# Chunked delta-rule scan in a diffusion step: second adaLN stage in another PSUM bank, chunk tiles without zeros, group norm squares on other engines

## Chip, cores and metric

One core of one Trainium2 chip runs the whole program. The metric is the device time of one execution in microseconds (us), lower is better; the median of three runs of the kernel before is given.

## What is computed

One inference step of a trunk of two layers over 128 context tokens and 512 latent tokens, width 1024. Layer 0 mixes tokens by a bidirectional delta-rule scan (RWKV-7) with 16 heads of 64, layer 1 by neighbourhood attention; behind each stands an MLP with squared ReLU. Every sub-layer is scaled, shifted and gated by six vectors (adaLN) that a matrix product makes from a conditioning vector. The scan, per head and direction, and what follows it:

```python
def step(S, inp):
    r_t, w_t, k_t, v_t, kk_t, a_t = inp
    sa = jnp.einsum('bhvk,bhk->bhv', S, -kk_t)
    S_new = (S * w_t[:, :, None, :] + sa[..., None] * (kk_t * a_t)[:, :, None, :]
             + v_t[..., None] * k_t[:, :, None, :]).astype(S.dtype)
    y = jnp.einsum('bhvk,bhk->bhv', S_new, r_t)
    return S_new, y
...
y = (ys[0] + ys[1]).astype(jnp.float32)
mean = jnp.mean(y, axis=-1, keepdims=True)
var = jnp.mean(jnp.square(y - mean), axis=-1, keepdims=True)
yn = ((y - mean) * lax.rsqrt(var + GN_EPS)).reshape(B, T, D) * ln_w + ln_b
...
sh1, sc1, gt1, sh2, sc2, gt2 = ada_mod(cond, ada_w[l], ada_b[l])
```

## The kernel before

The scan works in chunks of 32 tokens and holds 4 chunks of 5 blocks (one of context, four of latent tokens) for two directions d = 0, 1. `phase_scan` (from L770) loops over the blocks n and over four chunk steps e; in each, chain 0 and chain 1 advance by one chunk (`chain_step`, L1001), and between their parts `fill` (L881) slips in the preparation of a later block.

Preparation. For one unit (a block, one of two head groups hg, a direction, one of two windows) `prep_elem` (L899) loads decays and keys, sums the decays (L916, `wi`, on DVE, which is VectorE), takes two exponentials (L917, L918, ACT, which is ScalarE) and multiplies on POOL (GpSimd): KB, the write keys, and C (L947), the read keys. C has 128 partitions, 64 for each head of a pair (h = 0, 1); for head h the slots 8h to 8h+7 are filled on its own 64 partitions, and on the other 64 partitions they are set to zero (L939 on ACT for h = 1, L942 on POOL for h = 0). Slots 16 and 17 of C hold a 128x128 identity that `c_slots` (L728) writes once for each of the 16 C tiles. `prep_group` (L949) multiplies KB with C and the identity, 16 products to a group, two groups to a unit, into the PSUM tile `pp` (L852 is `mm`, which issues all products of the scan and chains them in program order). Then ACT copies a part to invA (L972) and the transposed write keys to C (L974), and DVE masks the rest into the zeroed half of C (L977), so that C can be multiplied over all 128 partitions. With eight units of a block done, `invert` (L979) inverts 32 triangular matrices at a time on DVE: a transpose (L985), 50 multiplications (L993) and 50 additions (L996), a transpose into TT (L998).

Chain. A chunk step is R = C x state into bank A (L852), copied by ACT to Rc (L1035); U = TT x Rc into bank A, copied by ACT into the state's tile GU (L1052); the state's update into bank B and its copy back to GU by ACT (L1108) or DVE with a decay (L1106, L1111); Y = C x GU into bank A, copied by ACT (L1069) or added by DVE (L1067). Each chain has one bank A, so R, U and Y of a chain use it one after the other. Each step also takes one block of 256 columns of the adaLN product: `ada_first` (into `pp`, copied to `adasb` at L289), and `ada_second` (L1046 calls it), two products of 2 columns and one DVE addition (L300, `mods`). They go to columns 256 to 259 of U's bank A of chain 1.

```python
        if self.ada_sums and d == 1:
            self.ada_second(*self.ada_sums.pop(0), ut[:, 256:260], self.mm)
        with tc.high_priority():
            for pp in range(2):
                for hp in range(2):
                    q = 2 * hp + pp
                    nc.scalar.activation(gu[64 - 64 * hp:96 - 64 * hp, hp, pp].rearrange("p b v -> p (b v)"),
                                         U[32 * q:32 * q + 32, :], AF.Copy, scale=-0.5)
```

Behind the chains `post_half` (L1114) normalises half a block of Y: mean (L1136) and subtraction (L1139), squares (L1140, ACT), their sum (L1142), an inverse root and the rest (L1146 to L1151) on DVE or POOL, whichever `el` is, a transpose on TensorE and two DVE products (L1160). `pbuf`, in which the squares lie, has one buffer for each pool; its other parts are loaded and stored by DMA.

The order of TensorE's instructions in the scan is the program's own; on the other engines a scheduler places them when the kernel is built, so that an edit moves rows on all engines.

Of the kernel before, what the change touches and what calls it, by code (L numbers as in the profile page):

```python
# [8 lines left out]
F32 = mybir.dt.float32  # L9
F32R = mybir.dt.float32r  # L10
I32 = mybir.dt.int32
AF = mybir.ActivationFunctionType
ALU = mybir.AluOpType
# [3 lines left out]
P = 128  # L17
# [155 lines left out]
class K:  # L173
# [554 lines left out]
    def c_slots(self, pool, n, par):  # L728

        for i in range(n):  # L730
            c = pool.tile([P, 26, 64], F32, name=f"C{i}")
            self.nc.any.tensor_copy(c[:, 16:18, :].rearrange("p a x -> p (a x)"), self.cst("ident"))
            self.free[par].append(c)
# [166 lines left out]
    def prep_elem(self, ts, hg, d, i):  # L900
# [34 lines left out]
        C = ts["C"][d, hg, ww] = self.free[ts["par"]].pop(0)  # L935
        for h in range(2):
            z = C[64 - 64 * h:P - 64 * h, 8 * h:8 * h + 8, :]
            if h:
                nc.scalar.activation(z.rearrange("p a b -> p (a b)"), self.cst("scan1")[64 - 64 * h:P - 64 * h, :512],  # L939
                                     AF.Copy, scale=0.0)  # L940
            else:
                nc.gpsimd.memset(z, 0.0)  # L942
        for s, f in ((0, f_at), (1, f_rt)):
# [5 lines left out]
    def prep_group(self, ts, hg, d, i, e):  # L949

        nc = self.nc
        ww = (i, 1 - i)[d]
        KB, C = ts["KB", hg, d, i], ts["C"][d, hg, ww]
        if e == 0:
            self.pa = self.pp_tile()
        pa = self.pa
        pv = pa.rearrange("p (e q x) -> p e q x", e=2, q=4)
        for q in range(4):
            for h in range(2):
                n = 8 * h + 4 * e + q  # L960
                r = 64 - 64 * h
                self.mm(pv[r:r + 64, e, q, :], lhsT=KB[:, q, e].rearrange("p s t -> p (s t)"), rhs=C[:, n:17 + h:16 + h - n, :],
                        start=True, stop=True, tile_position=(0, r))
        if e == 0:
            return
        if "D" not in ts:
            ts["D"] = self.inv.tile([P, 2, 8, 2, 32], F32, name="invA")
        mask = self.cst(f"amask{d}").unsqueeze(1).broadcast_to([P, 8, 64])
        pn = pa.rearrange("p (n x) -> p n x", x=P)
        for h in range(2):  # L970
            for b in range(2):
                nc.scalar.copy(ts["D"][32 * (2 * h + b):32 * (2 * h + b) + 32, d, 4 * hg + 2 * ww:4 * hg + 2 * ww + 2],  # L972
                               pv[64 - 64 * h:96 - 64 * h, :, b:4:2, 0:32])
        nc.scalar.copy(C[:, 18:26, :], pn[:, :, 64:P])  # L974
        for h in range(2):
            o = slice(64 - 64 * h, P - 64 * h)
            nc.vector.tensor_tensor(C[o, 8 * h:8 * h + 8, :], pn[o, :, 0:64], mask[o], op=ALU.mult)  # L977
# [23 lines left out]
    def chain_step(self, ts, n, e, d):  # L1001
# [21 lines left out]
        def state_product(s):  # L1023
            ps = self.ch.tile([P, 512], F32, name=f"A{d}")[:, :256]
            for ph, pp, hp in idx:
                q = 2 * hp + pp
                i = 8 * hp + 4 * ee + 2 * (ph % 2) + pp
                self.mm(ps[32 * q:32 * q + 32, 64 * ph:64 * ph + 64], lhsT=C[ph // 2][:, i, 32 * s:32 * s + 32],
                        rhs=gu[:, hp, pp, ph, :], start=True, stop=True, tile_position=(0, 32 * q))
            return ps  # L1030

        R = state_product(0)
        with tc.high_priority():
# [3 lines left out]
        TT = ts["TT"]  # L1037
        ut = self.ch.tile([P, 512], F32, name=f"A{d}")
        U = ut[:, :256]
        for ph, pp, hp in idx:  # L1040
# [4 lines left out]
                    rhs=Rc[qs, o], start=True, stop=True, tile_position=(32 * q, 32 * q))  # L1045
        if self.ada_sums and d == 1:  # L1046
            self.ada_second(*self.ada_sums.pop(0), ut[:, 256:260], self.mm)
        with tc.high_priority():
# [9 lines left out]
        yield  # L1058
        Y = state_product(1)
        tt = ts["tiles"][d]  # L1060
        with tc.high_priority():
            if tt not in self.yt:
                self.yt[tt] = self.yp.tile([P, 4, 256], F32, name="Y")
                self.ydone[tt] = set()
            yo = self.yt[tt][:, cq, :]
            if cq in self.ydone[tt]:
                nc.vector.tensor_tensor(yo, yo, Y, op=ALU.add)  # L1067
            else:
                nc.scalar.copy(yo, Y)  # L1069
                self.ydone[tt].add(cq)  # L1070
        if e % 2 == 1:
            self.free[ts["par"]] += [ts["C"].pop((d, hg, ww)) for hg in range(2)]
        yield

    def state_update(self, ts, n, e, d, gu, nx, C):
# [13 lines left out]
        for pp in range(2):  # L1089
            for ph in range(4):  # L1090
                for hp in range(2):
                    i = 18 + 4 * ee + 2 * (ph % 2) + pp
                    self.mm(G[hs(hp), pp, ph, :], lhsT=C[ph // 2][ho(hp), i, :], rhs=gu[ho(hp), hp, pp, ph, :],
# [20 lines left out]
    def post_half(self, tt, hb, on_dve):  # L1114
# [24 lines left out]
        el.tensor_tensor(Yg, Yg, bcast(sm), op=ALU.subtract)  # L1139
        nc.scalar.activation(sq, Yg, AF.Square)  # L1140
        var = po.tile([P, 8], F32, name="yvar")
# [456 lines left out]
```

## Time and profile before

| what | us |
|---|---|
| median of three runs | 2232.8 (2231.12 to 2234.78) |
| profiled execution | 2239.71 |
| its span, first to last instruction | 2237.9 |
| TensorE busy | 2011.6 (90%) |
| VectorE busy | 1169.5 (52%) |
| ScalarE busy | 857.0 (38%) |
| GpSimd busy | 455.1 (20%) |

The mean granted TensorE clock is 0.944. Preparation for the scan begins at about 288 us, the chains run from 400 to some 790 us, the output projection of the scan ends at some 842 us, and the rest is matrix products of MLP and attention. The busy times are sums over the whole span; where the scan's time goes is seen only by stretches.

### The profile page before, as it was taken

What the parts mean: (1) busy time and instruction counts of PE and PEld (TensorE: products, weight loads), DVE (VectorE), ACT (ScalarE), POOL (GpSimd) and SP (SyncE); (2) the same over time, 40 slices, a digit from 0 to 9 for tenths busy, and PEclk for the clock granted to TensorE, in tenths of its full rate; (3) what the DMA queues carried; (4) which work ended last, traced back from release to release, by engine and by line L of the source; (5) the groups of instructions that cost most, each with busy time, mean ns of one, the idle gap of its engine ahead of it and who ended that gap; (6) DMA issues with size and microseconds to landing.
All of it is one profiled execution on the core that took longest, in us unless ns stands there. A gap on an engine that the chain in (4) does not pass through costs nothing.

```text
span 2237.9 us, 44938 instructions
## 1 busy us (share of the span) xinstructions
PE 2011.6 (90%) x18604; PEld 1827.3 (82%) x18604; DVE 1169.5 (52%) x2592; ACT 857.0 (38%) x1712; POOL 455.1 (20%) x553
## 2 busy tenths in 40 slices
PE   6999988757665569999999999999999999999999
PEld 3777777646554568999999998889677999999999
DVE  6656658387679755433333434433666633434342
ACT  4544553546553414313131323221576331313130
POOL 0001275656542411101010110000232110101010
PEclk8997999978787788999999999999899999999999
DMA  6455764545433464323232223343310232222221
GB/s 242 147 157 155 229 205 135 173 133 166 129 132 96 112 187 141 105 76 111 72 111 76 86 76 119 132 135 92 110 57 31 75 122 76 76 76 76 76 74 69
DMA packets 161037, 260.03 MB, mean 116 GB/s; under 512 B 46528, under 2 KB 102976, under 8 KB 160832
## 3 DMA queue, kind: packets, MB, share of 16 engines
q1 hardware_dynamic: 152224, 244.05, 35.2%
q10 hardware_dynamic: 8608, 13.11, 1.7%
q8 instruction: 146, 2.39, 0.4%
q14 instruction: 59, 0.48, 0.1%
HBM read 218.18 MB, written 37.35 MB: 114 GB/s over the span
## 4 chain that ended last, share of the span: by engine, by line
PE 74%; DVE 13%; DMA 5%; POOL 3%; issue 2%; ACT 2%; SPq 1%; DVEq 0%; ACTq 0%; POOLq 0%
PE psl L205 54%; PE psl L239 3%; DVE invX L996 2%; PE ps L1525 2%; DVE invT L993 2%; POOL C L947 2%; PE po L1562 2%; PE pp L852 2%; PE pt L1550 2%; DVE C L977 1%; PE pp L1219 1%; PE psl L1265 1%; PE psl L286 1%; DMA ld_s<-scr 1%; PE A L852 1%
## 5 line engine op out<-in xcount | busy, mean ns | idle before, releaser
L191 ACT CAST whi<-wraw 128x1024 fp32r<-128x1024 f32 x178 | 186.6, 1049 | 731.5 <-PE psl L205 701.9
L205 PE MATMUL psl<-xh,whi 128*128 128x320 f32 (+1 forms) x1696 | 414.6, 317 | 9.6 <-ACT xh L247 4.9
L205 PE MATMUL psl<-xl,whi 128*128 128x320 f32 (+1 forms) x1696 | 410.2, 314 | 1.2 <-DVE xl L248 1.2
L205 PE MATMUL psl<-xh,wlo 128*128 128x320 f32 (+1 forms) x1696 | 409.7, 314 | 0.4 <-DVE ta L592 0.4
L205 PEld LDWEIGHTS psl<-xh,whi 128*128 128x128 f32 x1696 | 291.4, 191 | 28.5 <-issue 8.7
L205 PEld LDWEIGHTS psl<-xl,whi 128*128 128x128 f32 x1696 | 292.5, 191 | 5.7 <-issue 3.2
L205 PEld LDWEIGHTS psl<-xh,wlo 128*128 128x128 f32 x1696 | 292.9, 191 | 2.6 <-issue 1.7
L1172 DVE SCALAR_TENSOR_TENSOR xres<-psl,mods,xres 128x320 f32<-128x320 f32 (+2 forms) x216 | 81.7, 434 | 305.1 <-PE psl L205 305.1
L1345 POOL TENSOR_TENSOR relu<-relu 128x640 f32<-128x640 f32 x64 | 80.2, 1255 | 773.9 <-ACT relu L1344 758.7
L205 PE MATMUL psl<-hhl,whi 128*128 128x320 f32 x1024 | 233.1, 308 | 0.0
L205 PE MATMUL psl<-hhh,wlo 128*128 128x320 f32 x1024 | 233.0, 308 | 0.0
L205 PE MATMUL psl<-hhh,whi 128*128 128x320 f32 x1024 | 232.9, 308 | 0.0
L193 DVE TENSOR_TENSOR wlo<-wraw,whi 128x1024 fp32r<-128x1024 f32 x178 | 218.6, 1229 | 11.6 <-ACT whi L191 10.9
L205 PEld LDWEIGHTS psl<-hhh,whi 128*128 128x128 f32 x1024 | 170.8, 188 | 0.4 <-issue 0.4
L205 PEld LDWEIGHTS psl<-hhh,wlo 128*128 128x128 f32 x1024 | 171.1, 188 | 0.0
L205 PEld LDWEIGHTS psl<-hhl,whi 128*128 128x128 f32 x1024 | 171.0, 188 | 0.0
L1302 DVE TENSOR_TENSOR relu<-psl,rms_b 128x320 f32<-128x320 f32 x128 | 60.8, 486 | 144.6 <-PE psl L205 144.0
L852 PE MATMUL pp<-C,KB 128*64 128x128 f32 x1280 | 100.6, 306 | 39.7 <-DVE C L977 16.7
L852 PEld LDWEIGHTS pp<-C,KB 128*64 128x64 f32 x1280 | 83.0, 154 | 54.1 <-issue 28.8
L248 DVE TENSOR_TENSOR hhl<-relu,hhh 128x640 fp32r<-128x640 f32 x64 | 53.4, 834 | 127.9 <-ACT hhh L247 127.7
L1052 ACT ACTIVATE GU<-A 32x256 f32<-32x256 f32 x160 | 60.0, 375 | 93.2 <-DVE mods L300 64.0
L977 DVE TENSOR_TENSOR C<-pp,cstsb 64x512 f32<-64x512 f32 x80 | 55.0, 688 | 69.1 <-ACT C L974 56.9
(299 smaller groups left out, 3393.2 us busy)
## 6 DMA issues: line engine op xcount, KB each, us to landing
wraw<-in_mlp_w SPq DMA_DIRECT2D x128, 512.0 KB, 3.5
adaraw<-in_ada_w SPq DMA_DIRECT2D x96, 512.0 KB, 4.9
ld_d<-scr SPq DMA_DIRECT2D x20, 512.0 KB, 4.5
ld_s<-scr SPq DMA_DIRECT2D x20, 512.0 KB, 3.7
bias<-in_bias SPq DMA_DIRECT2D x16, 384.0 KB, 3.7
scr<-ta SPq DMA_DIRECT2D x16, 325.0 KB, 3.5
wi<-scr SPq DMA_DIRECT2D x20, 260.0 KB, 4.6
scr<-bp SPq DMA_DIRECT2D x16, 320.0 KB, 4.5
```

Source lines behind the costliest of these rows:

```text
L191: nc.scalar.copy(hi, raw)
L193: nc.vector.tensor_tensor(lo, raw, hi.bitcast(F32), op=ALU.subtract)
L205: self.nc.tensor.matmul(ps[g][:, :e - c], lhsT=a[:, k, :], rhs=b[:, c:e], start=(k == 0 and j == 0), stop=(k == n - 1 and j == 2))
L239: nc.tensor.matmul(ps, lhsT=a[:, tc_], rhs=w, start=(k == 0 and j == 0), stop=(k == KT - 1 and j == 2))
L248: (lo_eng or nc.vector).tensor_tensor(xl, src, xh.bitcast(F32), op=ALU.subtract)
L852: r = (op or self.nc.tensor.matmul)(*a, **k)
L947: nc.gpsimd.tensor_tensor(rev(o) if s == 0 else o, v4(sh, s, ww)[hs], f[hs], op=ALU.mult)
L977: nc.vector.tensor_tensor(C[o, 8 * h:8 * h + 8, :], pn[o, :, 0:64], mask[o], op=ALU.mult)
L1052: nc.scalar.activation(gu[64 - 64 * hp:96 - 64 * hp, hp, pp].rearrange("p b v -> p (b v)"), U[32 * q:32 * q + 32, :], AF.Copy, scale=-0.5)
L1172: nc.vector.scalar_tensor_tensor(out[:, a:b], ps[g][:, o:o + b - a], gate[:, k, j:j + 1], x[:, a:b], op0=ALU.mult, op1=ALU.add)
L1302: nc.vector.tensor_tensor(t[:, c], ps[q][:, :HALF], rb[:, c], op=ALU.mult)
L1345: nc.gpsimd.tensor_tensor(t, t, t, op=ALU.mult)
```

## The change

Four edits. (1) `ada_second` is called after Y, and its products go to columns 256 to 259 of Y's bank A; it was called after U. (2) C loses the zeroed halves: the ACT and POOL instructions that wrote them go, and the chunk products of head h run over the 64 partitions of h alone (`KB[hs]`, `C[hs]`), with the tile's row position 64h beside its column position. The mask's result (L977) is still written to the other half. (3) Instead of a 128x128 identity C holds one 64x64 identity for each half in one slot, which DVE adds together from two parts; the copied keys move from slot 18 to 17, and C has 25 slots. (4) The squares of the group norm are made by `el`, POOL or DVE, as the operations beside them.

```diff
-            c = pool.tile([P, 26, 64], F32, name=f"C{i}")
-            self.nc.any.tensor_copy(c[:, 16:18, :].rearrange("p a x -> p (a x)"), self.cst("ident"))
+            c = pool.tile([P, 25, 64], F32, name=f"C{i}")
+            self.nc.vector.tensor_tensor(c[:, 16], ident[:, :64], ident[:, 64:], op=ALU.add)
...
-        for h in range(2):
-            z = C[64 - 64 * h:P - 64 * h, 8 * h:8 * h + 8, :]
-            if h:
-                nc.scalar.activation(z.rearrange("p a b -> p (a b)"), self.cst("scan1")[64 - 64 * h:P - 64 * h, :512],
-                                     AF.Copy, scale=0.0)
-            else:
-                nc.gpsimd.memset(z, 0.0)
...
-                self.mm(pv[r:r + 64, e, q, :], lhsT=KB[:, q, e].rearrange("p s t -> p (s t)"), rhs=C[:, n:17 + h:16 + h - n, :],
-                        start=True, stop=True, tile_position=(0, r))
+                hs = slice(64 * h, 64 * h + 64)
+                self.mm(pv[r:r + 64, e, q, :], lhsT=KB[hs, q, e].rearrange("p s t -> p (s t)"), rhs=C[hs, n:17:16 - n, :],
+                        start=True, stop=True, tile_position=(64 * h, r))
...
-        nc.scalar.copy(C[:, 18:26, :], pn[:, :, 64:P])
+        nc.scalar.copy(C[:, 17:25, :], pn[:, :, 64:P])
...
-        if self.ada_sums and d == 1:
-            self.ada_second(*self.ada_sums.pop(0), ut[:, 256:260], self.mm)
...
+            if self.ada_sums and d == 1:
+                self.ada_second(*self.ada_sums.pop(0), pa[:, 256:260], self.mm)
...
-                    i = 18 + 4 * ee + 2 * (ph % 2) + pp
+                    i = 17 + 4 * ee + 2 * (ph % 2) + pp
...
-        nc.scalar.activation(sq, Yg, AF.Square)
+        el.tensor_tensor(sq, Yg, Yg, op=ALU.mult)
```

How it moves instructions, at three places. In the names, the figure after A, B or GU is the chain (A1 is bank A of chain 1), C0 to C7 are chunk tiles, and a last number counts the tile's uses; in brackets stand the engines or queues that a row waits for. The first is ACT in the first block's second chunk step, from the copy of R to that of U of chain 1. Before:

```order
L1035 COPY Rc_4285<-A1_4268 128x256 [waits PE_49]
L939 ACTIVATE C0_2648<-cstsb_60 64x512 [waits PE_49]
L1069 COPY Y_4097<-A0_4306 128x256 [waits PE_49]
L939 ACTIVATE C4_2656<-cstsb_60 64x512
L1052 ACTIVATE GU11_3897<-A1_4324 32x256 [waits DVE_49]
```

and now:

```order
L1031 COPY Rc_4253<-A1_4236 128x256 [waits PE_49]
L1062 COPY Y_4065<-A0_4274 128x256 [waits PE_49]
L1045 ACTIVATE GU11_3873<-A1_4292 32x256 [waits PE_49]
L1045 ACTIVATE GU11_3873<-A1_4292 32x256 x3
L918 ACTIVATE w_4925<-wi_4919 128x520 [waits DVE_49,Pool_49]
```

The zeros between the copies are gone, and the copy to GU waits for TensorE where it waited for DVE.

The second is DVE in the inversion for the second block, where the chains are in the third chunk step (e = 2) of the first: the rows around the sum of Y of chain 1 (A1_4802 before, A1_4759 now). Before:

```order
L977 TENSOR_TENSOR C4_2656<-pp0_4739,cstsb_60 64x512 [waits PE_49,Activation_49]
L977 TENSOR_TENSOR C4_2656<-pp0_4739,cstsb_60 64x512
L993 TENSOR_TENSOR invT0_4406<-invX_4402 128x210 [waits DVE_49]
L1067 TENSOR_TENSOR Y_4097<-Y_4097,A1_4802 128x256 [waits PE_49]
L996 TENSOR_TENSOR invX_4402<-invX_4402,invT0_4406 128x21x10 [waits DVE_49]
```

and now:

```order
L991 TENSOR_TENSOR invX_4363<-invX_4363,invT0_4367 128x10 [waits DVE_49]
L993 STREAM_TRANSPOSE TT_4469<-invX_4363 128x32x32 [waits DVE_49]
L917 SCALAR_TENSOR_TENSOR wi_5473<-cstsb_60,wi_5473 128x520 [waits DMAHW1_49,Pool_49]
L1060 TENSOR_TENSOR Y_4065<-Y_4065,A1_4759 128x256 [waits PE_49]
L300 TENSOR_TENSOR mods0_96<-A1_4759,parsb_58 128x4 [waits PE_49]
L972 TENSOR_TENSOR C2_2652<-pp1_4801,cstsb_60 64x512 [waits PE_49,Activation_49]
L972 TENSOR_TENSOR C2_2652<-pp1_4801,cstsb_60 64x512
```

The sum of Y stood within the inversion, behind 20 of its 100 multiplications and additions; it stands behind the last transpose now, and so do the `mods` of the same step and the masks of C2.

The third is TensorE at the same chunk step: Y of chain 1 and what follows it up to the next R of chain 1. Before:

```order
L852 MATMUL A1_4802<-GU10_2638,C3_2654 32x64 [waits DVE_49]
L852 MATMUL A1_4802<-GU10_2638,C3_2654 32x64 x7
L852 MATMUL A1_4802<-GU10_2638,C7_2662 32x64 x8
...
L852 MATMUL A1_4882<-GU11_3897,C3_2654 32x64 [waits DMAHW0_49,DVE_49]
```

and now:

```order
L853 MATMUL A1_4759<-GU10_2638,C3_2654 32x64 [waits PE_49]
L853 MATMUL A1_4759<-GU10_2638,C3_2654 32x64 x7
L853 MATMUL A1_4759<-GU10_2638,C7_2662 32x64 x8
L853 MATMUL A1_4759<-cstsb_60,adasb_4596 128x2 [waits DVE_49]
L853 MATMUL A1_4759<-cstsb_60,adasb_4596 128x2
...
L853 MATMUL A1_4842<-GU11_3873,C3_2654 32x64 [waits DMAHW0_49,DVE_49]
```

The two products of the second stage now stand behind Y; Y waits for DVE no longer, and the next R waits for DVE's readers of Y's bank.

## Rows read from the trace of the kernel before

**Rows 1.** Windows: stretch, us; PE, PEld, DVE, ACT, POOL busy (instructions); clock, DMA, GB/s.
```profile
395.00:443.70 48.70, 37.01 (x824) 29.22 (x826) 14.94 (x24) 26.57 (x70) 34.73 (x50) 0.93 0.61 178
443.70:494.70 51.00, 24.33 (x628) 19.55 (x620) 50.03 (x136) 22.98 (x57) 29.00 (x44) 0.79 0.46 141
494.70:527.30 32.60, 28.32 (x724) 21.85 (x724) 13.49 (x28) 22.15 (x59) 18.35 (x26) 0.91 0.46 147
527.30:579.80 52.50, 30.55 (x652) 24.93 (x652) 51.79 (x139) 21.67 (x57) 32.82 (x44) 0.70 0.49 143
579.80:611.80 32.00, 28.05 (x737) 22.56 (x740) 13.12 (x19) 23.02 (x61) 15.53 (x24) 0.90 0.45 143
611.80:651.20 39.40, 22.54 (x552) 18.95 (x546) 38.43 (x117) 17.65 (x48) 21.22 (x25) 0.83 0.35 112
651.20:685.70 34.50, 27.86 (x812) 21.96 (x806) 16.12 (x31) 21.64 (x59) 8.25 (x13) 0.95 0.48 155
685.70:725.70 40.00, 21.23 (x512) 17.19 (x512) 39.45 (x146) 11.73 (x25) 11.09 (x9) 0.70 0.30 85
```

**Rows 2.** Windows of line 996 alone (additions), first and last inversion of the four.
```profile
443.70:494.70 51.00, 17.78 (x50) 0.79 0.46 141
...
685.70:725.70 40.00, 15.04 (x50) 0.70 0.30 85
```

**Rows 3.** The same for line 993 (multiplications).
```profile
443.70:494.70 51.00, 15.66 (x50) 0.79 0.46 141
...
685.70:725.70 40.00, 13.28 (x50) 0.70 0.30 85
```

**Rows 4.** Groups of VectorE, 395 to 842 us: busy, mean ns, idle before.
```profile
L977 DVE TENSOR_TENSOR C<-pp,cstsb 64x512 f32<-64x512 f32 x56 | 38.5, 688 | 54.2 <-ACT C L974 42.6 <-PE A L852 6.9 <-ACT Rc L1035 3.7
...
L916 DVE TENSOR_TENSOR_SCAN wi<-cstsb,wi 128x520 f32<-128x520 f32 x11 | 13.9, 1266 | 17.7 <-DMA wi<-scr 10.6 <-POOL C L947 7.0
...
L998 DVE STREAM_TRANSPOSE TT<-invX 128x1024 f32<-128x1024 f32 x5 | 9.8, 1968 | 0.1
...
L1067 DVE TENSOR_TENSOR Y<-Y,A 128x256 f32<-128x256 f32 x20 | 8.3, 413 | 8.7 <-PE A L852 8.5
...
L1142 DVE TENSOR_REDUCE yvar<-pbuf 128x8 f32<-128x512 f32 x10 | 6.7, 679 | 2.9 <-ACT pbuf L1140 2.9
```

**Rows 5.** Waits of TensorE, 395 to 842 us: total, times, longest.
```profile
PE A L852 <- DVE rsq_t L262: 19.3, 1, 19.3
...
PE A L852 <- DVE TT L998: 14.1, 2, 12.8
```

**Rows 6.** Waits of ScalarE, the same stretch.
```profile
ACT GU L1052 <- DVE mods L300: 64.0, 15, 13.2
...
ACT pbuf L1140 <- DMA scr<-pbuf: 2.5, 1, 2.5
```

**Rows 7.** Groups of ScalarE, 395 to 791 us: zeros and squares.
```profile
L939 ACT ACTIVATE C<-cstsb 64x512 f32<-64x512 f32 x28 | 17.2, 628 | 0.7
...
L1140 ACT ACTIVATE pbuf<-Y 128x512 f32<-128x512 f32 x8 | 5.0, 628 | 21.1 <-POOL Y L1139 8.7 <-DMA bc<-scr 5.7 <-DVE rsq_i L259 2.6
```

**Rows 8.** Window in the front of the scan, columns as in rows 1.
```profile
299.00:368.00 69.00, 59.92 (x615) 52.76 (x615) 39.90 (x54) 36.59 (x95) 61.05 (x85) 1.00 0.51 158
```

**Rows 9.** Groups of GpSimd, whole trace.
```profile
L942 POOL MEMSET C<- 64x512 f32 x40 | 20.5, 522 | 7.2 <-PE A L852 4.8 <-PE psl L205 1.8 <-PE pk L698 0.2
...
L1139 POOL TENSOR_TENSOR Y<-Y,ysum 128x512 f32<-128x512 f32 x7 | 7.3, 1043 | 61.2 <-DVE ysum L1137 61.1
```

**Rows 10.** Timeline of TensorE, 409 to 414 us: start, length.
```profile
409.08 1.09 PE L852 MATMUL pp<-C,KB 128*64 128x128 f32 x16
...
411.70 1.15 PE L852 MATMUL B<-GU,C 64*64 64x64 f32 x32
412.78 0.65 PE L852 MATMUL A<-GU,C 128*32 128x64 f32 x32
413.36 0.65 PE L852 MATMUL A<-Rc,TT 32*32 32x64 f32 x32
```

More of the change, by code (lines that the diff above doesn't have):

```diff
@@ L728, in c_slots @@
     def c_slots(self, pool, n, par):
+        ident = self.cst("ident")
         for i in range(n):
-            c = pool.tile([P, 26, 64], F32, name=f"C{i}")
-            self.nc.any.tensor_copy(c[:, 16:18, :].rearrange("p a x -> p (a x)"), self.cst("ident"))
+            c = pool.tile([P, 25, 64], F32, name=f"C{i}")
+            self.nc.vector.tensor_tensor(c[:, 16], ident[:, :64], ident[:, 64:], op=ALU.add)
             self.free[par].append(c)
@@ L1023, in state_product @@
         def state_product(s):
-            ps = self.ch.tile([P, 512], F32, name=f"A{d}")[:, :256]
+            pa = self.ch.tile([P, 512], F32, name=f"A{d}")
+            ps = pa[:, :256]
             for ph, pp, hp in idx:
@@ L1029, in state_product @@
                         rhs=gu[:, hp, pp, ph, :], start=True, stop=True, tile_position=(0, 32 * q))
-            return ps
-        R = state_product(0)
+            return pa, ps
+        _, R = state_product(0)
         with tc.high_priority():
@@ L1037, in chain_step @@
         TT = ts["TT"]
-        ut = self.ch.tile([P, 512], F32, name=f"A{d}")
-        U = ut[:, :256]
+        U = self.ch.tile([P, 512], F32, name=f"A{d}")[:, :256]
         for ph, pp, hp in idx:
@@ L1058, in chain_step @@
         yield
-        Y = state_product(1)
+        pa, Y = state_product(1)
         tt = ts["tiles"][d]
```

## Prediction

> **What bounds the kernel now.** I read the windows by stage first, then the groups of VectorE and ScalarE, then who waits for whom, and the order of the instructions last. From 842 us to the end TensorE works almost without a gap and the change doesn't touch that part, so its worth is decided in the scan, 288 to 842 us. There the stretches alternate [rows 1]. In four of them VectorE is idle for over half the time (13 to 16 us busy of 32 to 49) and TensorE, but for the first of them, is busy for 28 us of 32 to 34.5: I call them T1. They run from one block's inverse TT to the next `invert`, and hold two chunk steps of both chains (e0 and e1) and the chunk products of the block to come. In the other four, T2, VectorE is busy for 97 to 99% (50.03 of 51.00, 51.79 of 52.50): that is the inversion, and TensorE works about half the time and shows a granted clock of 0.70 to 0.83, a mean of its two levels. The inversion's own multiplications and additions take 17.78 and 15.66 us in the first T2 and 15.04 and 13.28 in the last [rows 2, 3]; so some 16 us of the first T2 are other VectorE work that stands between them: masks of C (0.688 us each), scans of wi (1.27), sums of Y (0.41), reductions (0.68), and two transposes of 1.97 [rows 4]. TensorE waits for the end of it: 19.3 us once (named rsq_t, at the place where TT comes due) and 12.8 once [rows 5]. ScalarE waits 64.0 us for `mods` ahead of its copies to GU, the longest time 13.2 us [rows 6]; but what it waits for stands inside the same inversion, whose end decides anyway.
>
> **The change, part by part.** The sum is made against the profiled execution, 2239.7 us (span 2237.9 and 1.8 around it); the median of the runs is 2232.8, that is 6.9 less, and I take the difference over to it. About 4.5 us (0.2%) can be told from no change.
>
> *The second adaLN stage moves from U's bank to Y's.* ScalarE's copy to GU then waits for TensorE alone, and the wait for `mods` falls on the next R of chain 1, on TensorE, whose order in the scan is fixed: chunk products, B0, Y0 and U1 stand behind it. The order of the instructions shows where that bites. In the second block's inversion (the first T2 above), before, the sum of Y of e2 stands behind 20 of the 100 operations and its `mods` even earlier, so R1 of e3 could run inside; now the sum of Y and the `mods` of e2 both stand behind the last transpose, TT. So R1 of e3, and all of e3 behind it, falls to the following T1. The same holds in the next two T2. In the fourth, `mods` of e2 stays inside.
>
> *What leaves T2.* By the two orders, with the prices of [rows 4]: the first T2 loses 4 masks (2.75), 3 sums of Y (1.24), 2 scans (2.53) and 5 operations of 512 columns, priced at 0.68 as the reduction (3.4): 9.9 us. The second loses 4 masks and 4 rescalings, the latter priced as the mask (2.75 each), and gains two products of pbuf (0.83): 4.7. The third loses 2 masks: 1.4. The fourth loses one Y, one B, one reduction, one 512-wide operation and two products: 3.3. Sum **-19.3**. VectorE has room for these in T1 (it is idle there for 18 us and more), so they cost nothing where they go, unless TensorE waits for a mask there; I put that into the next term.
>
> *What T1 gains.* The first T1 after a T2 takes 32.6 us for two chunk steps and 1.7 us of R and Y, so a step is some 15.4 us; from R1 of e3 to its end I take a little over half, 8 us. Three times: **+24**. Ends: 6 each if ScalarE had run ahead, 15.4 if the whole step is left over.
>
> *Zeros.* Of 40 ScalarE zeros of 0.63 us, 28 stand in the chains, 17.2 us in all [rows 7]; with them go the short waits for `mods` in T1. TensorE's idle time in the four T1 is 11.7, 4.3, 4.0 and 6.6 us, 26.6 in all [rows 1], and that is the most that faster copies can give back there. I take **-10**, nearer to the zeros in T1 than to the whole; ends 0 and -17.2. The POOL memsets (0.522 us each [rows 9]) matter in front of the chains, where POOL is busy for 61.05 of 69.00 us [rows 8] and the 8 memsets there, 4.2 us, lie on its chain: **-3**, ends 0 and -5. Behind 400 us POOL has room, and I cost them at nothing; what covers them is the inversion.
>
> *The identity in the slot.* 16 VectorE additions of 128x64 take the place of 16 copies of 128x128, mostly before the chains begin. The nearest row is the sum of Y, 0.41 us for 256 columns [rows 4], so 16 of them are under 6.6 us, beside the v product of TensorE: 0, ends 0 and +2.
>
> *Products over 64 rows.* Their number and columns stay. Before, 16 of them take 1.09 us. The nearest rows with row tiles that alternate into one bank are B, 32 of half the columns in 1.15 us, and A from Rc and TT, 32 in 0.65, just what the other A takes with column tiles alone [rows 10]. By columns B is 36 ns for 64, the product 68 ns for 128. So **0**; ends -2 and, if they ran one after the other, twice 1.09 us per 16. The Trainium skill, page TensorEngine Tiling (Array Packing), section Gotcha 1: PSUM Pressure, speaks against this edit: different row tiles must write to different PSUM banks and cannot access one bank at the same time; by it the two halves of each pair here would take turns. By it the time would be that of the second rival below. The rows of B and A contradict it, since they do that already and are not slower.
>
> *Squares.* Ten squares leave ScalarE, which waited 21.1 us ahead of them, 8.7 of it for POOL and 10.8 in the tail behind 725 us (5.7, 2.6 and 2.5) [rows 6, 7]. There chains 0 and 1 stood behind them: **-3**, ends 0 and -10.8. In return 7 squares run on POOL, priced as its 512-wide operation at 1.04 us [rows 9], against 0.63 [rows 7], and VectorE waits for POOL at yvar, in T2 twice with the inversion queued behind it: **+1.5**, ends 0 and +7 x 1.04 = +7.3. A late pbuf transfer now holds POOL or VectorE instead of ScalarE.
>
> Sum: -19.3 + 24 - 10 - 3 - 3 + 1.5 = **-9.8 us**, so 2229.9 as a profiled execution and **2223** against the median.
>
> **The rivals.** *Slower: the wait behind the inversion.* The term of +24 is the weak one. The others make -33.8, so with 11.3 us of e3 left over in each of three periods the change gains nothing, and from there each further us costs 3. For it: R1 stands right behind the `mods`, with both chains' work after it, and the two `next` groups' masks are late as well. Against it: R0 and U0 of e3 stand ahead of R1. With 13 us, between my value and the whole step, the time is 2232.8 + 39 - 33.8 = 2238; with the whole step 2245. I put 2239, chance 0.18.
> *Slower by far: row tiles take turns.* By the order 34 masks lie in the four T1, one to each 16 products, where TensorE is nearly the bound; 1.09 us more for each gives +37 and some 2260. [Rows 10] speak against it: 0.03. This is what the Trainium skill's rule, cited above, would do.
> *No change.* Masks that leave T2 are waited for in T1, and what the inversion saves comes back behind it: 2233, chance 0.14. For it: VectorE's work in a period stays the same; against it: VectorE is idle for over half of T1.
> *A larger gain.* If the leftover of e3 costs only 6 us each, as the copies no longer wait, and ScalarE gives back 17.2: -19.3 + 18 - 17.2 - 4 - 3 = -25.5, and 2207. For it the 64.0 us of [rows 6]; against it TensorE's 28 busy of 32 us. Chance 0.13.
>
> **How the numbers follow.** The forecast, 2223, has 0.52; its own range, 2214 to 2232, holds the smaller ends (the tail, the front, 6 to 10 us for e3). The range of 8 in 10 takes in most of no change, of the larger gain and the nearer half of the slow case: 2206 to 2241. Faster by over 0.2% (under 2228.3): 0.45 of the forecast's 0.52, and the larger gain's 0.13: 0.58. Within 0.2%: 0.07 of the forecast, 0.13 of no change and a few hundredths of the slow case's near end: 0.23. Slower: 0.16 of the slow case and the row tiles' 0.03: 0.19.
>
> **What the next profile would show.** Right: in each T2 VectorE is still busy for over 95%, but the first takes 40 to 43 us and not 51; the T1 behind it takes 37 to 41 us and begins with R1, B0 and U1 of e3; waits of GU for `mods` are gone, and an idle time of TensorE at A, released by VectorE's `mods` or Y, stands ahead of R1; 16 products still take 1.09 us. Wrong: a T1 over 43 us (slow case), a T2 that keeps its 51 us (no change), 16 products that take 2 us at full clock (row tiles), or TensorE idle for less than 2 us in a T1 of 34 (the larger gain). If the front, 288 to 400 us, is not shorter by some 3 us, that term was wrong by itself.

## The result, and the profile after

The changed kernel takes 2293.5 us (median of five runs, 2286.8 to 2299.4) against 2232.9 for the kernel before (five runs beside them, 2231.1 to 2235.5): 1.0266 times as long [1.0242 to 1.0291], **60 us slower**. The prediction was 2223 with a range of 2206 to 2241, so it failed in sign and in size. The profiled execution took 2289.3 us, span 2287.5, mean granted clock 0.929.

The windows by stage of the changed kernel, one TensorE-fed T1 and one T2 (an inversion) by turns, with the columns of [rows 1]:

```profile
390.80:446.06 55.26, 34.98 (x800) 27.94 (x800) 11.92 (x20) 21.69 (x58) 26.24 (x40) 0.81 0.49 145
446.06:483.05 36.99, 12.90 (x304) 11.02 (x300) 34.23 (x115) 10.48 (x27) 14.89 (x18) 0.71 0.31 97
483.05:542.99 59.94, 44.90 (x1043) 35.37 (x1047) 26.03 (x47) 30.10 (x79) 32.43 (x46) 0.84 0.43 136
542.99:586.20 43.21, 21.78 (x424) 16.98 (x424) 41.21 (x132) 13.57 (x35) 22.82 (x23) 0.72 0.38 109
586.20:641.22 55.02, 35.41 (x978) 30.34 (x980) 18.18 (x29) 27.53 (x75) 24.29 (x36) 0.81 0.44 138
641.22:678.90 37.68, 19.61 (x386) 16.03 (x384) 34.87 (x114) 13.02 (x34) 14.64 (x19) 0.66 0.30 95
678.90:725.83 46.93, 33.68 (x942) 28.00 (x938) 19.79 (x39) 22.56 (x64) 12.90 (x18) 0.86 0.43 142
725.83:764.80 38.97, 20.47 (x464) 16.21 (x464) 37.27 (x134) 10.18 (x25) 12.94 (x10) 0.63 0.29 86
```

Against [rows 1] the four T2 fell from 182.90 to 156.85 us, so -26.1. The four T1 rose from 147.80 to 217.15, so +69.4. TensorE's column tells what these are made of. Its busy time in T2 fell from 98.65 to 74.76 (-23.9) and rose in T1 from 121.24 to 148.97 (+27.7): work that ran beside the inversion now runs behind it. Its idle time stayed the same in T2 (84.3 and 82.1) and rose in T1 from 26.6 to 68.2 (+41.6). So T1 took on 27.7 us of TensorE's work, nearly all of it moved there (3763 instructions against 3097), and 41.6 of new idle time.

The chains' progress says it more simply. One Y, copied by ScalarE or added by VectorE, ends each step of one chain. Counted in the timelines of the two engines from the `invert`'s first transpose to TT, the kernel before ends 4, 4, 3 and 4 chain steps inside its four T2 and 4 in each T1. The changed kernel ends 1, 2, 2 and 3 inside T2, and 4, 7, 6 and 5 in T1. Sixteen chain steps in T1 became 22. By the same marks T1 grew from 155.7 to 225.0 us, 9.7 and 10.2 us for each chain step. The front of the scan is shorter, as predicted (the first TT starts at 388.74 us, before at 393.08), but one execution of each doesn't show a gain of this size: over all kernels of this document the first TT lies between 386.2 and 393.7 us without the zeros and between 387.7 and 396.2 with them. Between the first and last TT 43.4 us were lost, and behind the last TT some 10.5 (1524.6 us to the end of the span, before 1514.1), where ten chain steps end and not nine. Less the 4.3 us of the front, these make the 49.6 us by which the two profiled spans differ; the medians differ by 60.6, as the profiled execution of before lies 6.8 us above its median and that of the changed kernel 4.2 below.

Waits of the changed kernel, 395 to 842 us (total, times, longest), which answer to [rows 5, 6]; none for `rsq_t` or TT is left among them:

```profile
ACT GU L1045 <- PE A L853: 72.3, 29, 14.3
...
ACT w L918 <- DVE wi L917: 57.7, 5, 13.5
DVE wi L917 <- DMA wi<-scr: 43.0, 9, 14.9
...
PE A L853 <- DVE Y L1060: 39.9, 8, 13.4
...
PE A L853 <- ACT Rc L1031: 29.4, 6, 8.9
PE A L853 <- ACT Y L1062: 29.1, 10, 15.1
```

The copies to GU wait for TensorE and no longer for `mods`, as predicted; TensorE waits for the readers of Y. The timelines of TensorE, then of VectorE and of ScalarE in the changed kernel (start, length, and in brackets the idle time ahead) show where:

```profile
404.20 1.09 PE L853 MATMUL pp<-C,KB 64*64 64x128 f32 x16
...
413.26 1.10 PE L853 MATMUL A<-GU,C 128*32 128x64 f32 x64
429.44 1.02 PE L853 MATMUL A<-cstsb,adasb 128*128 128x2 f32 x4 [15.08 <-ACT Y L1062]
430.38 1.08 PE L853 MATMUL A<-Rc,TT 32*32 32x64 f32 x32
431.39 1.97 PE L853 MATMUL pp<-C,KB 64*64 64x128 f32 x16
...
469.91 1.10 PE L853 MATMUL A<-GU,C 128*32 128x64 f32 x64
484.45 1.01 PE L853 MATMUL A<-cstsb,adasb 128*128 128x2 f32 x4 [13.43 <-DVE Y L1060]
```

```profile
423.33 1.24 DVE L917 TENSOR_TENSOR_SCAN wi<-cstsb,wi 128x520 f32<-128x520 f32 x1 [14.91 <-DMA wi<-scr]
...
481.14 1.91 DVE L993 STREAM_TRANSPOSE TT<-invX 128x1024 f32<-128x1024 f32 x1
...
484.00 0.40 DVE L1060 TENSOR_TENSOR Y<-Y,A 128x256 f32<-128x256 f32 x1
```

```profile
424.60 0.64 ACT L918 ACTIVATE w<-wi 128x520 f32<-128x520 f32 x1 [13.48 <-DVE wi L917]
...
429.00 0.38 ACT L1062 COPY Y<-A 128x256 f32<-128x256 f32 x1
```

The two holes have different origins. The first, ahead of 429.44, is in T1: VectorE's scan waits 14.91 us for its load, ScalarE's exponential 13.48 for the scan, and the copy of Y stands behind the exponential. The second, ahead of 484.45, fills the end of the first T2. At 469.91 R of e3 (chain 0) and Y of e2 (chain 1) are done in one go; the next thing in TensorE's order is the adaLN products, which go into Y's bank, so they wait for the sum of Y, and that stands behind TT. U of e3, with everything after it, waits behind them. Behind a hole TensorE is also slower. Windows ahead of, in and behind the first one:

```profile
404.00:414.00 10.00, 10.00 (x276) 7.39 (x272) 1.38 (x2) 5.29 (x14) 3.45 (x4) 1.00 0.57 158
...
414.00:430.00 16.00, 0.92 (x31) 0.76 (x19) 2.62 (x3) 4.58 (x11) 9.76 (x16) 0.61 0.39 124
...
430.00:435.00 5.00, 5.00 (x69) 3.48 (x70) 1.29 (x2) 1.50 (x4) 0.00 (x0) 0.54 0.21 75
```

The granted clock was 1.00 (2.4 GHz) before it and 0.54, near 1.2 GHz, behind it; 16 products took 1.09 us at 404 and 1.97 at 431. Over the four T1 it was 0.81 to 0.86, against 0.90 to 0.95 in [rows 1].

In the groups of TensorE in the changed kernel (busy, mean ns | idle ahead; the first from 395 to 842 us, the second of the whole trace) the two edits of its work look like this:

```profile
L853 PE MATMUL A<-cstsb,adasb 128*128 128x2 f32 x64 | 12.6, 301 | 61.5 <-DVE Y L1060 32.4 <-ACT Y L1062 29.1
```

```profile
L853 PE MATMUL pp<-C,KB 64*64 64x128 f32 x1280 | 103.0, 311 | 32.9 <-DVE C L972 13.4 <-POOL C L941 12.2 <-DVE invX L991 4.7
```

The 61.5 us of idle time ahead of the adaLN products are so near to the 60 lost that they look like the answer. By the experiments they are worth about a sixth of it.

### The profile page after: what moved, and what is told of

It reads as the page before. It is cut to its first block, busy times and chain, and to the rows that moved or that the text cites. A ratio compares the mean times of both kernels' runs of the same rounds, so it can differ in the third digit from the quotient of the medians.

```text
span 2287.5 us, 44848 instructions
## 1 busy us (share of the span) xinstructions
PE 2021.2 (88%) x18604; PEld 1837.5 (80%) x18604; DVE 1167.5 (51%) x2605; ACT 831.1 (36%) x1652; POOL 444.4 (19%) x520
## 4 chain that ended last, share of the span: by engine, by line
PE 71%; DVE 10%; DMA 7%; POOL 6%; issue 4%; ACT 2%; SPq 1%; ACTq 0%; DVEq 0%; POOLq 0%
PE psl L205 53%; POOL C L941 4%; PE psl L239 3%; PE ps L1520 2%; DVE invX L991 2%; PE po L1557 2%; DVE invT L988 2%; DMA wi<-scr 2%; PE pt L1545 2%; PE psl L1260 1%; DMA ld_s<-scr 1%; DMA adaraw<-in_ada_w 1%; PE A L853 1%; PE pp L853 1%; PE psl L286 1%
## 5 line engine op out<-in xcount | busy, mean ns | idle before, releaser
L853 PE MATMUL pp<-C,KB 64*64 64x128 f32 x1280 | 103.0, 311 | 32.9 <-DVE C L972 13.4
L853 PEld LDWEIGHTS pp<-C,KB 64*64 64x64 f32 x1280 | 85.1, 155 | 48.9 <-POOL C L941 17.1
L853 PE MATMUL A<-GU,C 128*32 128x64 f32 x2560 | 59.8, 247 | 40.5 <-DVE mods L300 12.9
```

Source lines behind the costliest of these rows:

```text
L853: r = (op or self.nc.tensor.matmul)(*a, **k)
```

## The experiments

The kernel before ran again beside each set, at medians of 2238.0 to 2241.0 us; every ratio is to those runs.

**One part at a time.** The first four put the adaLN call back, or make one edit alone: the call; the chunk tiles (no zeros, 64 rows, identity in the slot); the squares.

The call back behind U in the changed kernel:

```diff
+        if self.ada_sums and d == 1:
+            self.ada_second(*self.ada_sums.pop(0), ut[:, 256:260], self.mm)
...
-            if self.ada_sums and d == 1:
-                self.ada_second(*self.ada_sums.pop(0), pa[:, 256:260], self.mm)
```

The second does the reverse to the kernel before; the third and fourth are edits (2) with (3), and (4), of the change as they stand in its diff, made alone.

> The kernel after, with the second adaLN stage called after U again; all else as in the change. Theory P (the two adaLN products behind Y wait for Y's reader on ScalarE or VectorE and hold TensorE's fixed order): all of the 61 us of TensorE's idle time ahead of them goes, and the time falls from 2293.5 to 2222-2240. Theory E (the loss is the scan's exponentials, which stand one group of copies earlier on ScalarE now and hold the chain's copies while wi is still under way): their place is the same here, so the time stays above 2265.

> The kernel before with only the second adaLN stage moved behind Y. Theory P: TensorE idles 40 to 60 us ahead of the two products, 2270-2295. Theory E: the exponentials keep their place of before, so within 10 us of 2233. My prediction's own mechanism (only mods read late, the rest of e3 pushed behind the inversion): 2233-2245.

> The kernel before with only the chunk tiles without zeros, the products over 64 rows and the 64x64 identity. Theory P: no loss, a gain from the zeros of 5 to 20 us, 2213-2228. Theory E: the exponentials stand one group earlier in four places, at some 10 us each, 2265 or more. Row tiles taking turns in one bank: 16 products take over 1.5 us at full clock, and 2260 or more.

> The kernel before with only the squares moved to POOL and VectorE. All theories: small. By the waits of 21 us ahead of ScalarE's squares 2222-2233; if POOL's longer square holds VectorE at yvar, up to 2240.

Measured: the changed kernel with the call back at U 2289.4 us, 1.0214 [1.0166, 1.0261]; the call alone 2251.4, 1.0061 [1.0040, 1.0082]; the chunk tiles alone 2284.4, 1.0198 [1.0165, 1.0231]; the squares alone 2240.7, 1.0004 [0.9982, 1.0025]. So the adaLN call costs 12 to 14 us by itself. On top of the chunk tiles it costs some 10 (60.6 us lost with it and 50.4 without), which is not clear of the noise, as the intervals of the two ratios overlap. The 2251.4 lies outside all three ranges expected for that run. The chunk tiles bring the rest. The group of the adaLN products with the call alone:

```profile
L852 PE MATMUL A<-cstsb,adasb 128*128 128x2 f32 x64 | 11.5, 283 | 38.8 <-ACT Y L1068 22.3 <-DVE Y L1066 16.4
```

38.8 us idle ahead of them, and 12 lost: idle time ahead of an instruction is not the loss that it causes. That the next instruction would have had to wait as well is the likely reason; it was not tested.

**Which part of the chunk tiles, and which wait.** In this order: the rows edit alone on the kernel before, the zeros and the identity kept; on the changed kernel POOL's copy FC ordered behind the last KB, as SP's loads waited 109.7 us for KB; on the changed kernel one exponential of each unit ordered behind a later copy of C; and on the kernel before the adaLN call ahead of Y's reader.

```diff
-                self.mm(pv[r:r + 64, e, q, :], lhsT=KB[:, q, e].rearrange("p s t -> p (s t)"), rhs=C[:, n:17 + h:16 + h - n, :],
-                        start=True, stop=True, tile_position=(0, r))
+                self.mm(pv[r:r + 64, e, q, :], lhsT=KB[hs, q, e].rearrange("p s t -> p (s t)"), rhs=C[hs, n:17 + h:16 + h - n, :],
+                        start=True, stop=True, tile_position=(64 * h, r))
...
+                self.behind(fcp, self.last_kb)
...
+                self.behind(wx, self.evs[-3])
...
         pa, Y = state_product(1)
+        if self.ada_sums and d == 1:
+            self.ada_second(*self.ada_sums.pop(0), pa[:, 256:260], self.mm)
```

> The kernel before with nothing but the products over 64 rows: zeros, identity, squares and the adaLN stage as before. The products take 1.09 us per 16 at full clock in the runs so far, as before, so theory R (they cost more on TensorE) gives nothing here by durations. Theory E (the scheduler's order of the preparation on ScalarE, POOL and SyncE is what costs; it has changed here too, the exponentials stand one group earlier in three places): 2260 to 2290. Theory Z (the missing zeros matter, as they had held the preparation back): within 10 us of before.

> The kernel after with one ordering on POOL: the copy FC of a new unit stands behind the last product KB of the unit before; the exponentials keep their place on ScalarE. Theory E-POOL (KB waits behind FC, FC for the exponential, and SyncE's load of ld_d for KB, with wi and the chains' v behind it): SyncE's 110 us of waiting for KB falls under 50 and the time to 2240-2260. Theory E-ACT (the exponentials' own place on ScalarE costs): stays at 2285-2295.

> The kernel after with one ordering on ScalarE: the exponentials of a new unit stand behind the copy of C that is two before the newest one at that point of the program, at least a group later than in the change. Theory E-ACT: ScalarE's waits of 58 us for wi fall under 25 and the time to 2235-2260. Theory E-POOL: FC still stands ahead of KB and KB gets later with it, 2285 or more.

> The kernel before with the second adaLN stage in Y's bank, but its products straight behind those of Y, ahead of the copy that reads Y. Theory P (in the run with the stage behind the copy the two products waited for Y's reader and held TensorE, and this was its whole loss of 12 us): no wait is left ahead of the products, 2228-2242. Rival (the loss there is the mods read late, inside or behind the inversion, as I had predicted): 2245-2255 again.

Measured: the rows edit alone 2292.4 us, 1.0242 [1.0218, 1.0265]; FC behind KB 2289.5, 1.0225 [1.0202, 1.0248]; exponentials later 2286.4, 1.0208 [1.0185, 1.0232]; adaLN ahead of the reader 2239.3, 0.9989 [0.9974, 1.0004]. The rows edit is the whole loss of the chunk tiles. The waits of SP for KB and of ScalarE for `wi` are not most of it. They were nearly gone in the second and the third run (395 to 842 us; 109.7 and 57.7 in the changed kernel):

```profile
SPq L919 <- POOL KB L942: 0.8, 1, 0.8
```

```profile
ACT w L924 <- DVE wi L923: 10.3, 1, 10.3
```

The time lost stayed at 48.5 and 45.5 us. The second of these has an interval that lies below that of the changed kernel (60.6 lost, another set), so up to some 15 us may hang on ScalarE's waits. And the adaLN products cost nothing once they stand ahead of Y's copy:

```profile
L852 PE MATMUL A<-cstsb,adasb 128*128 128x2 f32 x64 | 9.7, 256 | 0.0
```

**The products themselves, or the order they bring.** The rows edit changes no count of instructions, but the scheduler that places them at build time puts others in their places: 627 of VectorE's 2592 positions hold another instruction, 136 of ScalarE's 1682, 98 of POOL's 556, 93 of SP's 738 and 170 of TensorE's 14284. These kernels hold every engine to a written list of instruction numbers, by dependencies that order and nothing else:

```diff
+def pin_all(tc, kept):
+    for line in ORDER.split("\n"):
+        last = None
+        for w in line.split():
+            i = kept.get("I-" + w)
...
+            if last:
+                tc.add_manual_dep(i, last, mybir.DependencyInfo(
+                    mybir.DependencyClass.NoSync, mybir.DependencyReason.DATA), reason="order")
+            last = i.name
```

> As the run with the products over 64 rows alone, but with every engine and queue held to the order of the kernel before, instruction for instruction. Theory O (the scheduler's new order is the whole loss): 2233-2248. Theory R (row tiles that alternate in one bank cost the time on the chip, in a way that the durations do not show): 2280-2297 again.

> The kernel before, products over 128 rows as they were, with every engine and queue held to the order that the run with 64 rows had. Theory O: 2280-2297. Theory R: 2233-2248.

> The kernel before with all of the chunk tile edit (no zeros, products over 64 rows, 64x64 identity), the common instructions of all engines held to the order of the kernel before. Theory O: the loss of 45 us goes and what the zeros are worth is left, 2218-2240. Theory R: 2275 or more.

> As the run before this one and the squares on POOL and VectorE: the change without the adaLN move, in the order of the kernel before. Theory O: 2215-2240; if it lies under 2230 the two edits are a version faster than both kernels. Theory R: 2275 or more.

Measured: the rows edit in the order of before 2237.8 us, 0.9990 [0.9976, 1.0003]; **the unchanged kernel in the order of the rows edit 2289.5, 1.0226 [1.0195, 1.0257]**; all of the chunk tiles' edits in the order of before 2237.3, 0.9995 [0.9975, 1.0015]; the same with the squares moved 2244.4, 1.0024 [1.0010, 1.0039], a little above the range expected. So the 50 us are the order, and the products over 64 rows are free. The group of the rows edit in the order of before (whole trace):

```profile
L1593 PE MATMUL pp<-C,KB 64*64 64x128 f32 x1280 | 105.0, 313 | 41.0 <-DVE C L1593 19.0 <-POOL C L1593 11.3 <-DVE invX L1593 8.5
```

What the order does is seen in VectorE's timeline in the first T2, of the rows edit in the order of before (in these kernels one line records all; of its four sums of Y there the last two are shown):

```profile
475.22 0.42 DVE L1593 TENSOR_TENSOR Y<-Y,A 128x256 f32<-128x256 f32 x1
475.77 0.15 DVE L1593 TENSOR_TENSOR mods<-A,parsb 128x4 f32<-128x4 f32 x1
...
481.98 0.41 DVE L1593 TENSOR_TENSOR Y<-Y,A 128x256 f32<-128x256 f32 x1
...
495.88 1.93 DVE L1593 STREAM_TRANSPOSE TT<-invX 128x1024 f32<-128x1024 f32 x1
```

and of the unchanged kernel in the order of the rows edit:

```profile
473.19 0.40 DVE L1592 TENSOR_TENSOR Y<-Y,A 128x256 f32<-128x256 f32 x1
...
488.56 1.91 DVE L1592 STREAM_TRANSPOSE TT<-invX 128x1024 f32<-128x1024 f32 x1
490.34 0.39 DVE L1592 TENSOR_TENSOR Y<-Y,A 128x256 f32<-128x256 f32 x1
...
494.74 0.42 DVE L1592 TENSOR_TENSOR Y<-Y,A 128x256 f32<-128x256 f32 x1
495.07 0.15 DVE L1592 TENSOR_TENSOR mods<-A,parsb 128x4 f32<-128x4 f32 x1
```

Of the four sums of Y that stood among the inversion's 100 operations one is left there; the others, and the last `mods`, stand behind TT. TT is 7 us earlier, and three chain steps are left over. Its windows of the first T1 and T2 look like those of the changed kernel:

```profile
397.20:453.25 56.05, 36.55 (x809) 28.61 (x807) 12.29 (x19) 26.27 (x67) 30.78 (x46) 0.82 0.50 142
453.25:490.50 37.25, 20.07 (x373) 15.50 (x372) 35.96 (x116) 13.44 (x36) 15.08 (x21) 0.68 0.37 120
```

Counted as above, its chain steps inside T2 are 1, 2, 2 and 3, those of the three kernels in the order of before 4, 4, 3 and 4.

**Which engines' order.** The lists of two engines from the rows edit, the other three from before. VectorE's and ScalarE's lists were not tried one without the other.

> The kernel before with the order that the run with 64 rows had on POOL and SyncE alone; ScalarE, VectorE and TensorE stay in the order of before. Theory O-queues (POOL's FC ahead of KB, and SyncE's loads behind KB, make the loss): 2275-2297. Theory O-ACT/DVE (it is where the inversion, the masks, the exponentials and the chains' copies stand against each other): 2233-2250.

> The kernel before with the order that the run with 64 rows had on ScalarE and VectorE alone; POOL, SyncE and TensorE stay in the order of before. Theory O-ACT/DVE: 2275-2297, and the stretches from one TT to the next inversion are 50 us or more, as in the change. Theory O-queues: 2233-2250.

Measured: POOL and SP 2263.1 us, 1.0114 [1.0058, 1.0169], with 4, 4, 3 and 4 chain steps in T2; ScalarE and VectorE 2280.2, 1.0189 [1.0144, 1.0234], with 1, 2, 2 and 3. The shift of chain steps is thus made by the order on ScalarE and VectorE, and it costs 42 us without the rest. POOL's and SP's order costs 25 in another way, mostly through longer T2 (189.2 us in all, 175.0 before), and lies between the two ranges expected. VectorE's waits for the load of `wi` are 33.3 us there and 10.6 before; what they cost was not tested. The two losses do not add up: they make 67 by themselves and 50 together.

**Early exponentials and scans.** In the bad order the exponentials (L917, L918) and the scans (L916) of some units stand so early that they wait for their loads. The next four put them behind the neighbours that they have in the kernel before: the exponentials, in the full order and in that of ScalarE and VectorE alone, and then exponentials and scans of the same units, in the same two orders.

The first unit's two exponentials in ScalarE's list, and its scan in VectorE's (of the 22 exponentials 15 change their place by this; of the scans those of eight units were to go back, of which five change their place, and those of three others were left):

```diff
 4098
-4576
 4119
...
 4122
-4577
 4140
...
 4187
+4576
 4205
+4577
 4223
```

```diff
 4032
-4575
 4118
 4145
 4146
+4575
 4969
```

> The kernel before in the order of the 64-row run, as in the run that gave 2289, with one thing put back: ScalarE's exponentials of the eleven units prepared beside the chains stand where they stood before; 22 instructions on one engine. Theory X (ScalarE's wait for wi at these exponentials, with the chain's copies behind, is the core of it): ScalarE's waits for wi fall from about 57 us under 30, and the time to 2240-2262. Theory D (it is VectorE's order, with the chain's operations outside the inversion): 2275-2295.

> As the run with ScalarE and VectorE alone in the order of the 64-row run, which gave 2280, with the same 22 exponentials back at their places. Theory X: 2233-2255. Theory D: 2268-2285.

> The kernel before in the slow order of the 64-row run on all engines, with VectorE's scans of wi and ScalarE's exponentials back at their places of before for eight of the eleven units (the other three cannot be moved without a circle of waits). Theory S (the late load of wi holds whichever engine has its reader early in its queue; with both readers back nothing of the chain stands behind it): VectorE's waits for wi fall from 43-49 us under 20 and the time to 2240-2265. Theory D (VectorE's order around the inversion costs by itself): 2275-2295.

> The same with POOL, SyncE and TensorE in the order of before, so that ScalarE and VectorE alone stand in the slow order, without the early scans and exponentials. Theory S: 2233-2252. Theory D: 2265-2290.

Measured: 2289.5 us, 1.0221 [1.0166, 1.0275]; 2289.3, 1.0225 [1.0182, 1.0268]; 2301.6, 1.0276 [1.0250, 1.0301]; 2289.5, 1.0238 [1.0206, 1.0270]. None gains, the third lies above both ranges expected, and all four keep 1, 2, 2 and 3. With the exponentials back (ScalarE and VectorE order) the hole in the first T1 stays, since VectorE itself waits for the load, first its own row and then TensorE's:

```profile
429.46 1.24 DVE L1592 TENSOR_TENSOR_SCAN wi<-cstsb,wi 128x520 f32<-128x520 f32 x1 [13.26 <-DMA wi<-scr]
```

```profile
431.99 2.37 PE L1592 MATMUL B<-GU,cstsb 128*64 128x512 f32 x4 [12.70 <-ACT GU L1592]
```

With the scans back too (the same two lists), the first T1 is 50.9 us, from 58.9 in the run of these lists as they were and 56.2 with the exponentials back. But the four T2 grow from 143.7 to 156.1 us in all, and ScalarE's timeline still has long waits for `mods`, four of about 15 us and more, one for each T2 (two of them shown; 92.1 us in all, 64.0 before):

```profile
462.88 1.57 ACT L1592 ACTIVATE GU<-A 32x256 f32<-32x256 f32 x4 [16.05 <-DVE mods L1592]
...
571.85 1.57 ACT L1592 ACTIVATE GU<-A 32x256 f32<-32x256 f32 x4 [17.68 <-DVE mods L1592]
```

These runs do not take the late loads out, though. VectorE's waits for them were to fall under 20 us, but they grew: with the scans early they are 33.4 us in the full order and 32.1 in that of the two lists (395 to 842 us), with the scans back, in these two orders, and then in the kernel before:

```profile
DVE wi L1592 <- DMA wi<-scr: 54.9, 10, 10.2
```

```profile
DVE wi L1592 <- DMA wi<-scr: 43.9, 10, 9.1
```

```profile
DVE wi L916 <- DMA wi<-scr: 10.6, 3, 4.7
```

So the order on ScalarE and VectorE makes 42 us, and which rows of it do so is not shown. The likely ones are the chains' own rows on VectorE around the inversion (sums of Y, `mods`, masks, rescalings). The counts of all 18 runs agree with that: every kernel with a median of 2280 us or more ends 8 or 9 chain steps in its four T2, every one with VectorE and ScalarE in the order of before 15. But the count does not set the time by itself: the kernel with the adaLN products ahead of Y's copy ends 19 and is no faster than the one before, and that with POOL's and SP's order ends 15 and loses 25 us. Moving the chains' rows alone was not tried, and scans that wait for late loads stay a rival. No kernel here beats the one before.

## Why the prediction was wrong

- **T2, -19.3.** Right in kind: -26.1 in the windows. The reason given, that operations leave the inversion for T1, was right too: VectorE's busy time fell by 32.1 us in T2 and rose by 18.3 in T1.
- **"They cost nothing where they go".** This is the step that failed. I priced the leaving operations as VectorE time, of which T1 has plenty. But a sum of Y and its `mods` are also links of a chain. Behind TT they hold back the chain steps that ran beside the inversion for nothing: 15 steps ended in T2 before and 8 now, T1 grew by 69.4 us, and a T1 over 43 us, the sign named for the slow case, came in all four (46.9 to 59.9; before, 48.7 in the first and 32.0 to 34.5 in the others). The run of the unchanged kernel in the order of the rows edit shows that the order alone does this; how much of it is the chains' rows and how much the rows that wait for late loads stays open.
- **"R1 of e3, and all of e3 behind it ... 8 us. Three times: +24".** The mechanism, chain steps left over behind TT, was named for this term and as the slow rival, and the counts bear it out; its size was wrong. Three times somewhat over half of a two-chain step is some three steps of one chain; seven left T2, six for T1 and one for the stretch behind the last TT. T1 gained 69.4 us, where the sum had 14 (+24 and -10), and 41.6 of the 69.4 are idle time of TensorE. Part of this is the wait for loads in T1 (the first hole above), which the sum did not have. I had read the new order at the places where the change was, at e3 of a block, and taken the rest of it as before. "R0 and U0 of e3 stand ahead of R1" was no comfort: the adaLN products, waiting for the sum of Y behind TT, stand ahead of U0.
- **The adaLN wait** was put on the next R of chain 1. It falls mostly on the adaLN products themselves, earlier in TensorE's order, and as a wait for Y's readers: 61.5 us idle ahead of them, and 12.9 for `mods`. By itself the move costs 12 us, on top of the rest some 10 (not clear of the noise), and by itself nothing if the call stands ahead of Y's copy.
- **Products over 64 rows, 0.** Right: 2237.8 us against 2239.3 with the order held, 313 ns against 306 for one. By my estimate taking turns would have cost 37 us. Gotcha 1: PSUM Pressure, in the page TensorEngine Tiling (Array Packing) of the Trainium skill, says that different row tiles write to different banks and cannot access one bank at the same time. Here two row tiles did write to one bank, each to its own half of the partitions (row position 64h, column position 64 - 64h), and ran at the old speed; two row tiles in the same partitions of a bank were not run.
- **Zeros -10, memsets -3.** Wrong: with the order held, leaving the zeros out gives 0.9995 [0.9975, 1.0015]. The front of the changed kernel is 4.3 us shorter in the profiled executions, within the scatter told above; with the order of before no gain is seen at the end.
- **Squares -3 + 1.5.** Alone no difference (1.0004); on top of the chunk tiles, with the order held, 7 us slower (1.0024 against 0.9995, with intervals that just overlap). The upper end had +7.3.
- **The chances.** The slow side had 0.19, most of it at 2239, because I bounded the leftover of e3 by one step of 15.4 us. The profile of before did not exclude more: 15 chain steps ended inside T2, their rows on VectorE among those of the inversion.

## What to carry to other kernels

Where a scheduler sets the order, an edit that looks local can move everything: compare the new order over the whole stretch, and count how many steps of the critical chain it ends under each long operation (a sign to look further, as the runs with 19 and 15 show, and not the time itself). Price an operation that is moved by what waits for it, not by the room at the place where it goes. To tell an edit from its order, hold the order and make the edit, and hold the edit back and take its order: here that split 50 us into 0 and 50.

## What the runs showed of the hardware

The same instructions on the same data, in another order on each engine, differ by 50 us, 2.3% of the whole. The longest idle time ahead of one group of TensorE's instructions, 61.5 us, was worth only some 10 us when it was taken away (50.4 us lost against 60.6, each to the kernel before in its own set; the intervals overlap). Fp32 products of two row tiles into one bank, each to its own half of the partitions, took 313 ns each, against 306 over 128 rows.
